# One-hot columns moved from GpSimd to VectorE and ScalarE, v tiles split one step earlier, rows fetched three slots ahead

## The chip, the cores and the metric

The kernel runs on one core of a Trainium2 chip. The metric is the device time of one execution in microseconds (us). The engines of the core run their own instruction queues in order and wait for each other through semaphores: TensorE (PE in the rows; PEld are its weight loads), VectorE (DVE), ScalarE (ACT), GpSimd (POOL), and SyncE (SP), which here only issues transfers. Sixteen DMA engines carry the transfers.

## What is computed

The reference is one layer of an encoder with 1024 tokens of width 1024: an attention group and an RWKV-7 group, their output projection, and a feed-forward part called PEER, which retrieves single-neuron experts by product keys. The change lies in PEER alone:

```python
# per token: 8 heads x 16 chosen experts = 128 indices ib and gates gb out of 128*128 experts
def block(args):                       # xc: 128 tokens, ic: their indices, gc: their gates
    xc, ic, gc = args
    u = jnp.take(expert_u, ic, axis=0)
    act = jax.nn.gelu(jnp.einsum('cd,ced->ce', xc, u), approximate=False)
    vv = jnp.take(expert_v, ic, axis=0)
    return jnp.einsum('ce,ced->cd', gc * act, vv)
```

## The kernel before

PEER is done in two ways side by side. For the first 3 blocks of 128 tokens (`NGB` = 3) the chosen rows of U and V are fetched from HBM by indirect DMA, one row for each token and slot: 384 slots, each one fetch `gu` and one fetch `gv` of 128 x 1024 fp32, issued by GpSimd (`fetch`, L1362). VectorE multiplies `gu` with the token's `ghr` and sums (L1390), and adds `gv` times the activation onto `gacc` (L1398), 16 slots later. For the other 5 blocks (640 tokens) all 16384 experts are computed densely, in 128 tiles of 128 experts: `act_half` makes the activations of a tile (48 matmuls, `pact`, L315 to L317), a gate zeroes those that were not chosen, and `v_steps` multiplies them with V. Each fp32 operand is split into a high part (ScalarE copy) and a low part (VectorE subtraction): `uTh`/`uTl`, `ah`/`al`, `vh`/`vl`, and each product is three matmuls.

**The gates stage** (`g_steps`) makes the gate tables. For each of 640 tokens, 128 slots on the partitions, `o2` is the one-hot of an expert's low 7 bits and `o1` the one-hot of its high 7 bits times its gate; the matmul `o1` by `o2` (L1733, `pgb`) is the token's 128 x 128 table of gates. One step `hot(t8)` makes the one-hots of 8 tokens, `mm(t8)` their 8 products; ScalarE evicts them into `st` (L1736), and SyncE stores `st` to `Gd` in HBM. There are 80 such steps, with two buffers (`NHOT` = 2) of `o1` and of `o2`. Before the change the 8 columns of `o1` are shared out by `MIX = "DDDDPPAA"`: four on VectorE and two on GpSimd (L1712, compare and multiply in one), two on ScalarE (L1718 and L1722, as relu(gate - gate * |x - index|)). `tT` holds the transposed indices and gates. Dense tiles (`A(e2, NEARLY)`) and 60 fetched slots (`NG3`) are laid between these steps.

**The last stage** goes over the 32 groups of 4 tiles. A group has 8 steps, one for each tile and half of the output (`one`): 15 matmuls `py` (L1827 to L1829) with `vh`, `vl`. After the last of 4 steps VectorE adds the 5 sums `py` onto `yac` (L1836), which frees their PSUM. In the same 8 steps the next group's activations are gated: `gate` multiplies `gl` by the table `gt_` on GpSimd (L1786), then come `ah` (ScalarE, L1787) and `al` (VectorE, L1788). Activations that were computed early come back from HBM (`gl<-actd`, L1776, SyncE), the others from `act_half`. `vr` tiles are loaded four steps ahead (`NVR` = 4 buffers), `vh` and `vl` have three buffers (`NV`). Fetches are tied behind GpSimd's latest gate or one-hot (`pace`).

The order of the instructions on each engine is not that of the code: a scheduler works it out before the run, from priorities in program order and estimated times, and from when buffers come free.

Of the kernel before, what the change touches and what calls it, by code (L numbers as in the profile page):

```python
# [8 lines left out]
F32 = mybir.dt.float32  # L9
# [4 lines left out]
AF = mybir.ActivationFunctionType  # L14
ALU = mybir.AluOpType
# [5 lines left out]
D = 1024  # L21
# [23 lines left out]
NPOP = 2  # L45
NHOT = 2
NXG = 3
LAG = 2
GD = 2
VAH = 0  # L50
NVR = 4
TRY = (1, 1)
WG = (1, 0, 0.99)
# [14 lines left out]
TC = 32  # L68
NSTB = 2
STQ = 0  # L70
MIX = "DDDDPPAA"
HD = 64


# [5 lines left out]
def body(tc, nc, I, out, dbg=None):  # L80
# [3 lines left out]
    with root:  # L84
# [76 lines left out]
        def acp(o_, i_):  # L161
            nc.scalar.activation(o_, i_, AF.Copy)  # L162
# [56 lines left out]
        for k in range(NK):  # L219
            for i in range(2):  # L220
                a = slot("adw")
# [10 lines left out]
        for tb in range(NB):  # L232
# [5 lines left out]
            if tb % 4 == 3:  # L238
                r_ = rstd[:, tb - 3:tb + 1]
# [1049 lines left out]
        for tb in range(NB):  # L1289
# [7 lines left out]
            if tb % 2:  # L1297
                r_ = ss2[:, tb - 1:tb + 1]
                nc.vector.tensor_scalar(r_, r_, 1.0 / D, 1e-6, op0=ALU.mult, op1=ALU.add)
                rsqrt(r_, r_, [128, 2], "r1")  # L1300
                for b in range(tb - 1, tb + 1):
                    h_ = tl[f"h{b}"]
                    for hf in range(2):
                        cs_ = slice(hf * 512, hf * 512 + 512)
                        nc.vector.scalar_tensor_tensor(h_[:, cs_], h2[b][:, cs_], ss2[:, b:b + 1], sc2[hf],
                                                       op0=ALU.mult, op1=ALU.mult)
# [113 lines left out]
        pace = [None]  # L1420
# [253 lines left out]
        with ES() as gs:  # L1674
# [7 lines left out]
            def g_steps(b):  # L1682
# [3 lines left out]
                def prep():  # L1686
                    ij = g1.tile([128, 2, 128], I32, name="ij", bufs=1)
                    nc.vector.tensor_scalar(ij[:, 0], eid[tb], 7, None, op0=ALU.logical_shift_right)
                    nc.vector.tensor_scalar(ij[:, 1], eid[tb], 127, None, op0=ALU.bitwise_and)
                    fj = g1.tile([128, 2, 128], F32, name="fj", bufs=1)  # L1690
                    nc.vector.tensor_copy(fj, ij)
                    pt = pg_.tile([128, 512], F32, name="ptg", tag="b")
                    nc.tensor.transpose(pt[:, 0:128], fj[:, 0], ident)
                    nc.tensor.transpose(pt[:, 128:256], fj[:, 1], ident)
                    nc.tensor.transpose(pt[:, 256:384], wgt[tb], ident)

                    s["t"] = tT = g1.tile([128, 5, 128], F32, name="tT")
                    acp(tT[:, 0:3].rearrange("p a b -> p (a b)"), pt[:, 0:384])
                    nc.scalar.activation(tT[:, 3], pt[:, 256:384], AF.Copy, scale=-1.0)
                    nc.scalar.activation(tT[:, 4], pt[:, 0:128], AF.Copy, scale=-1.0)  # L1700

                def hot(t8):
                    tT = s["t"]
                    t0 = t8 * 8
                    s[t8] = o1, o2 = [g1.tile([128, 8, 128], F32, name=n_, bufs=NHOT) for n_ in ("o1", "o2")]
                    nc.vector.tensor_tensor(o2, io128[:, None, :].to_broadcast([128, 8, 128]),
                                            tT[:, 1, t0:t0 + 8, None].to_broadcast([128, 8, 128]), ALU.is_equal)
                    for q in range(8):
                        t = t0 + q
                        if MIX[q] != "A":  # L1710
                            eng = nc.vector if MIX[q] == "D" else nc.gpsimd
                            r_ = eng.tensor_scalar(o1[:, q], io128, tT[:, 0, t:t + 1], tT[:, 2, t:t + 1],  # L1712
                                                   op0=ALU.is_equal, op1=ALU.mult)
                            if MIX[q] == "P":
                                pace[0] = r_
                        else:

                            nc.scalar.activation(o1[:, q], io128, AF.Abs, bias=tT[:, 4, t:t + 1])  # L1718
                    for q in range(8):
                        t = t0 + q  # L1720
                        if MIX[q] == "A":
                            nc.scalar.activation(o1[:, q], o1[:, q], AF.Relu, scale=tT[:, 3, t:t + 1],  # L1722
                                                 bias=tT[:, 2, t:t + 1])

                def mm(t8):
                    if t8 % (TC // 8) == 0:
# [189 lines left out]
```

## Time and profile before

| | |
|---|---|
| Median of 3 runs | 3918.12 us (3916.42 to 3923.77) |
| The profiled execution | 3917.25 us, span of its instructions 3915.5 us |
| Granted TensorE clock, mean | 0.925 |
| TensorE busy | 3337.0 us (85%) |
| VectorE busy | 3016.5 us (77%) |
| GpSimd busy | 1929.2 us (49%) |
| ScalarE busy | 1248.9 us (32%) |

Durations and waits come from the profiled execution. "Busy" is the time in which at least one instruction of the engine ran; matmuls are pipelined, so a busy TensorE is not one at its peak. A wait is put down to the instruction or the DMA that released it last.

### The profile page before, as it was taken

The numbers are of one execution on the slowest core, as the hardware profiler recorded it, in microseconds if no ns is written. First come the engines' busy times: TensorE is split into PE (matmuls) and PEld (weight loads), VectorE is DVE, ScalarE is ACT, GpSimd is POOL, SyncE is SP. The second block draws the span as 40 slices with busy tenths as digits, with TensorE's granted clock in tenths as the row PEclk, the third lists the DMA queues.
The fourth block names the chain that finished last, engine by engine and source line by source line (L and its number), as shares of the span: only waits on it lengthen the run. The fifth ranks groups of instructions, "written<-read, shape, count | busy, mean of one in ns | idle before, by whom it ended". The sixth has DMA issues, their size and how long they took to land. (4 is left out here: it accounts for less than half of the span.)

```text
span 3915.5 us, 59807 instructions
## 1 busy us (share of the span) xinstructions
PE 3337.0 (85%) x21937; PEld 2929.5 (75%) x21937; DVE 3016.5 (77%) x6210; ACT 1248.9 (32%) x2400; POOL 1929.2 (49%) x1506
## 2 busy tenths in 40 slices
PE   5968899899697978878778777898999889998898
PEld 4747877777586978878777776777777777777777
DVE  6785557667647899999988886777777877788776
ACT  3234344445213322222355552222222222222221
POOL 2132111221334365456799996555555655555541
PEclk9988999899798988998999898999999999999999
DMA  6443434443455366566688889777777877777774
GB/s 198 178 135 123 141 95 121 101 105 94 110 185 190 97 213 219 170 218 227 209 287 282 280 288 328 285 282 290 294 292 293 300 284 290 295 297 298 291 269 158
DMA packets 493454, 862.68 MB, mean 220 GB/s; under 512 B 149348, under 2 KB 290404, under 8 KB 489064
## 3 DMA queue, kind: packets, MB, share of 16 engines
q1 hardware_dynamic: 372840, 447.20, 35.3%
q0 software_dynamic: 113280, 411.63, 28.9%
q8 instruction: 173, 2.83, 0.3%
q10 hardware_dynamic: 7040, 0.03, 0.1%
q14 instruction: 121, 0.99, 0.1%
HBM read 741.91 MB, written 116.80 MB: 219 GB/s over the span
## 5 line engine op out<-in xcount | busy, mean ns | idle before, releaser
L317 PE MATMUL pact<-dTh,uTl 128*128 128x320 f32 x2048 | 650.3, 319 | 51.6 <-DVE uTl L1450 51.4
L315 PE MATMUL pact<-dTh,uTh 128*128 128x320 f32 x2048 | 652.6, 319 | 10.1 <-ACT gl L1461 6.1
L316 PE MATMUL pact<-dTl,uTh 128*128 128x320 f32 x2048 | 648.3, 317 | 0.0
L1390 DVE SCALAR_TENSOR_TENSOR gu<-gu,ghr 128x1024 f32<-128x1024 f32 x384 | 505.0, 1316 | 162.8 <-DMA gu<-in_peer_u_dram,ei 150.4
L1827 PE MATMUL py<-vh,ah 128*128 128x512 f32 x1280 | 523.7, 410 | 93.1 <-DVE yac L1836 64.3
L1398 DVE SCALAR_TENSOR_TENSOR gacc<-gv,gact,gacc 128x1024 f32<-128x1024 f32 x381 | 533.3, 1400 | 72.4 <-DMA gv<-in_peer_v_dram,ei 67.5
L1828 PE MATMUL py<-vl,ah 128*128 128x512 f32 x1280 | 527.6, 412 | 64.1 <-DVE vl L1807 63.5
L1362 POOL DMA_INDIRECT gu<-in_peer_u_dram,ei x384 | 504.0, 1313 | 123.6 <-issue 65.8
L1829 PE MATMUL py<-vh,al 128*128 128x512 f32 x1280 | 519.8, 406 | 3.7 <-DVE al L1788 3.7
L1362 POOL DMA_INDIRECT gv<-in_peer_v_dram,ei x384 | 457.4, 1191 | 131.4 <-issue 103.0
L317 PEld LDWEIGHTS pact<-dTh,uTl 128*128 128x128 f32 x2048 | 397.9, 195 | 58.3 <-DVE uTl L1450 58.2
L315 PEld LDWEIGHTS pact<-dTh,uTh 128*128 128x128 f32 x2048 | 398.9, 195 | 15.5 <-ACT gl L1461 8.0
L316 PEld LDWEIGHTS pact<-dTl,uTh 128*128 128x128 f32 x2048 | 398.6, 195 | 2.5
L1827 PEld LDWEIGHTS py<-vh,ah 128*128 128x128 f32 x1280 | 252.9, 198 | 154.9 <-issue 37.0
L1828 PEld LDWEIGHTS py<-vl,ah 128*128 128x128 f32 x1280 | 253.8, 198 | 140.0 <-DVE vl L1807 88.9
L1829 PEld LDWEIGHTS py<-vh,al 128*128 128x128 f32 x1280 | 253.5, 198 | 58.2 <-DVE al L1788 4.5
L1806 ACT ACTIVATE vh<-vr 128x512 fp32r<-128x512 f32 x256 | 156.0, 625 | 392.3 <-PE py L1829 361.9
L1733 PE MATMUL pgb<-o,o 128*128 128x128 f32 x1280 | 194.7, 300 | 80.7 <-POOL o L1712 76.8
L1712 POOL TENSOR_SCALAR o<-io,tT 128x128 f32<-128x128 f32 x160 | 244.5, 1533 | 11.7 <-ACT tT L162 9.3
L1733 PEld LDWEIGHTS pgb<-o,o 128*128 128x128 f32 x1280 | 174.3, 208 | 97.3 <-POOL o L1712 92.3
L1787 ACT ACTIVATE ah<-gl 128x640 fp32r<-128x640 f32 x128 | 91.2, 735 | 439.6 <-POOL gl L1786 302.9
L1788 DVE TENSOR_TENSOR al<-gl,ah 128x640 fp32r<-128x640 f32 x128 | 103.7, 830 | 130.3 <-ACT ah L1787 130.3
(1443 smaller groups left out, 7244.7 us busy)
## 6 DMA issues: line engine op xcount, KB each, us to landing
u<-in_peer_ut_dram SPq DMA_DIRECT2D x128, 512.0 KB
vr<-in_peer_v_dram SPq DMA_DIRECT2D x256, 256.0 KB
Gd<-st SPq DMA_DIRECT2D x160, 256.0 KB
actd<-gl SPq DMA_DIRECT2D x65, 320.0 KB
gl<-actd SPq DMA_DIRECT2D x65, 320.0 KB
awt<-in_ada_w_dram SPq DMA_DIRECT2D x32, 512.0 KB
wraw<-in_peer_w_query_dram SPq DMA_DIRECT2D x32, 512.0 KB
wraw<-in_w_in_dram SPq DMA_DIRECT2D x26, 512.0 KB
```

Of the source, the lines that this page charges most:

```text
L315: nc.tensor.matmul(ps, lh, rh, start=(i == 0), stop=False)
L316: nc.tensor.matmul(ps, lh, rl, start=False, stop=False)
L317: nc.tensor.matmul(ps, ll, rh, start=False, stop=(i == n - 1))
L1362: g_ = nc.gpsimd.indirect_dma_start(out=r_, out_offset=None, in_=src, in_offset=bass.IndirectOffsetOnAxis(ap=eid[tb][:, j:j + 1], axis=0))
L1390: nc.vector.scalar_tensor_tensor(u, u, 1.0, hr, op0=ALU.mult, op1=ALU.mult, accum_out=act[:, q:q + 1])
L1398: nc.vector.scalar_tensor_tensor(acc, v, pact[:, q:q + 1], acc, op0=ALU.mult, op1=ALU.add)
L1712: r_ = eng.tensor_scalar(o1[:, q], io128, tT[:, 0, t:t + 1], tT[:, 2, t:t + 1], op0=ALU.is_equal, op1=ALU.mult)
L1733: nc.tensor.matmul(pg[:, q * 128:(q + 1) * 128], o1[:, 4 * x_ + q], o2[:, 4 * x_ + q], start=True, stop=True)
L1806: nc.scalar.activation(vh, vts[i], AF.Copy)
L1827: nc.tensor.matmul(ys[hf][b], ah[:, ts], vh, start=(n == tiles[0]), stop=False)
L1828: nc.tensor.matmul(ys[hf][b], ah[:, ts], vl, start=False, stop=False)
L1829: nc.tensor.matmul(ys[hf][b], al[:, ts], vh, start=False, stop=(n == tiles[-1]))
```

## The change

Three things change. In the gates stage `MIX` goes: VectorE makes both one-hots of 8 tokens as whole comparisons, `o1` first, without the gates, and ScalarE then multiplies each of the 8 columns of `o1` by its gate (a copy with a pointer scale, in place). GpSimd makes no columns there, and so the fetches of that stage are no longer tied behind one. `tT` shrinks from five blocks to three. `VAH` = 1: in each step of the last stage the code splits the v tile of the next step. `LAG` = 3: the code fetches the rows of three slots ahead of the slot in work, with the buffers as they were (four of `gu` and of `gv`, three more in the gates stage).

```diff
--- before.py
+++ after.py
@@ -45,9 +45,9 @@
 NPOP = 2
 NHOT = 2
 NXG = 3
-LAG = 2
+LAG = 3
 GD = 2
-VAH = 0
+VAH = 1
 NVR = 4
 TRY = (1, 1)
 WG = (1, 0, 0.99)
@@ -68,7 +68,6 @@
 TC = 32
 NSTB = 2
 STQ = 0
-MIX = "DDDDPPAA"
 HD = 64
 
 
@@ -1694,33 +1693,19 @@
                     nc.tensor.transpose(pt[:, 128:256], fj[:, 1], ident)
                     nc.tensor.transpose(pt[:, 256:384], wgt[tb], ident)
 
-                    s["t"] = tT = g1.tile([128, 5, 128], F32, name="tT")
-                    acp(tT[:, 0:3].rearrange("p a b -> p (a b)"), pt[:, 0:384])
-                    nc.scalar.activation(tT[:, 3], pt[:, 256:384], AF.Copy, scale=-1.0)
-                    nc.scalar.activation(tT[:, 4], pt[:, 0:128], AF.Copy, scale=-1.0)
+                    s["t"] = tT = g1.tile([128, 3, 128], F32, name="tT")
+                    acp(tT.rearrange("p a b -> p (a b)"), pt[:, 0:384])
 
                 def hot(t8):
                     tT = s["t"]
                     t0 = t8 * 8
                     s[t8] = o1, o2 = [g1.tile([128, 8, 128], F32, name=n_, bufs=NHOT) for n_ in ("o1", "o2")]
-                    nc.vector.tensor_tensor(o2, io128[:, None, :].to_broadcast([128, 8, 128]),
-                                            tT[:, 1, t0:t0 + 8, None].to_broadcast([128, 8, 128]), ALU.is_equal)
+
+                    for i, o_ in enumerate((o1, o2)):
+                        nc.vector.tensor_tensor(o_, io128[:, None, :].to_broadcast([128, 8, 128]),
+                                                tT[:, i, t0:t0 + 8, None].to_broadcast([128, 8, 128]), ALU.is_equal)
                     for q in range(8):
-                        t = t0 + q
-                        if MIX[q] != "A":
-                            eng = nc.vector if MIX[q] == "D" else nc.gpsimd
-                            r_ = eng.tensor_scalar(o1[:, q], io128, tT[:, 0, t:t + 1], tT[:, 2, t:t + 1],
-                                                   op0=ALU.is_equal, op1=ALU.mult)
-                            if MIX[q] == "P":
-                                pace[0] = r_
-                        else:
-
-                            nc.scalar.activation(o1[:, q], io128, AF.Abs, bias=tT[:, 4, t:t + 1])
-                    for q in range(8):
-                        t = t0 + q
-                        if MIX[q] == "A":
-                            nc.scalar.activation(o1[:, q], o1[:, q], AF.Relu, scale=tT[:, 3, t:t + 1],
-                                                 bias=tT[:, 2, t:t + 1])
+                        nc.scalar.activation(o1[:, q], o1[:, q], AF.Copy, scale=tT[:, 2, t0 + q:t0 + q + 1])
 
                 def mm(t8):
                     if t8 % (TC // 8) == 0:
```

The scheduler's order shows what moves. **ScalarE in the gates stage**, in its second half; `o` are the one-hots, `st<-pgb` the evictions of the products, `gl<-pact` a dense activation. Before:

```order
L1736 ACTIVATE st<-pgb 128x128x4 x2
L1718 ACTIVATE o_21379<-io_11962,tT 128x128 x2
L1722 ACTIVATE o_21379<-o_21379,tT 128x128 x2
L1736 ACTIVATE st<-pgb 128x128x4 x2
L1718 ACTIVATE o_21412<-io_11962,tT 128x128 x2
L1722 ACTIVATE o_21412<-o_21412,tT 128x128 x2
L1736 ACTIVATE st<-pgb 128x128x4 x2
L1461 ACTIVATE gl<-pact 128x320
```
After the change:

```order
L1708 ACTIVATE o_21622<-o_21622,tT 128x128 x8
L1708 ACTIVATE o_21640<-o_21640,tT 128x128 x8
L1721 ACTIVATE st<-pgb 128x128x4 x4
L1460 ACTIVATE gl<-pact 128x320
L1708 ACTIVATE o_21700<-o_21700,tT 128x128 x8
L1708 ACTIVATE o_21726<-o_21726,tT 128x128 x8
L1721 ACTIVATE st<-pgb 128x128x4 x4
L1460 ACTIVATE gl<-pact 128x320
```
Four instructions on two columns become eight on eight columns, and two such groups stand behind each other more often, ahead of the evictions of both.

**VectorE in the last stage**, from the last `yac` of one half of a group to the row product behind the two `al` (buffer numbers tell a row: `gu_26924` is one fetch). Before:

```order
L1836 TENSOR_TENSOR yac4_22458<-yac4_22458,py_26675 128x512
L1807 TENSOR_TENSOR vl_26906<-vr_26746,vh_26905 128x512
L1390 SCALAR_TENSOR_TENSOR gu_26884,gact_26547<-gu_26884,ghr_22005 128x1024
L1398 SCALAR_TENSOR_TENSOR gacc_22926<-gv_26886,gact_25807,gacc_22926 128x1024
L1807 TENSOR_TENSOR vl_26941<-vr_26773,vh_26940 128x512
L1450 TENSOR_TENSOR uTl_27097<-u_26890,uTh_27096 128x1024
L1788 TENSOR_TENSOR al_26897<-gl_26805,ah_26896 128x640
L1788 TENSOR_TENSOR al_27000<-gl_26936,ah_26999 128x640
L1807 TENSOR_TENSOR vl_26970<-vr_26863,vh_26969 128x512
L1390 SCALAR_TENSOR_TENSOR gu_26924,gact_26547<-gu_26924,ghr_22005 128x1024
L1398 SCALAR_TENSOR_TENSOR gacc_22926<-gv_26926,gact_25807,gacc_22926 128x1024
```
After the change:

```order
L1821 TENSOR_TENSOR yac4_22372<-yac4_22372,py_26593 128x512
L1792 TENSOR_TENSOR vl_26784<-vr_26664,vh_26783 128x512
L1792 TENSOR_TENSOR vl_26824<-vr_26691,vh_26823 128x512
L1389 SCALAR_TENSOR_TENSOR gu_26802,gact_26465<-gu_26802,ghr_21927 128x1024
L1397 SCALAR_TENSOR_TENSOR gacc_22844<-gv_26804,gact_25725,gacc_22844 128x1024
L1449 TENSOR_TENSOR uTl_27015<-u_26808,uTh_27014 128x1024
L1773 TENSOR_TENSOR al_26815<-gl_26723,ah_26814 128x640
L1773 TENSOR_TENSOR al_26918<-gl_26854,ah_26917 128x640
L1792 TENSOR_TENSOR vl_26859<-vr_26781,vh_26858 128x512
L1389 SCALAR_TENSOR_TENSOR gu_26842,gact_26465<-gu_26842,ghr_21927 128x1024
L1397 SCALAR_TENSOR_TENSOR gacc_22844<-gv_26844,gact_25725,gacc_22844 128x1024
```
The second `vl` moves ahead of a pair of row products; what stands behind it is in the same order. The fetches of these rows on GpSimd, before:

```order
L1362 DMA gu_26884<-in_peer_u_dram,ei1_11947 128x1024
L1362 DMA gv_26886<-in_peer_v_dram,ei1_11947 128x1024
L1786 TENSOR_TENSOR gl_26936<-gl_26936,gt__26901 128x640
L1786 TENSOR_TENSOR gl_26805<-gl_26805,gt__26518 128x640
L1362 DMA gu_26924<-in_peer_u_dram,ei1_11947 128x1024
```
After the change:

```order
L1361 DMA gu_26802<-in_peer_u_dram,ei1_11947 128x1024
L1361 DMA gv_26804<-in_peer_v_dram,ei1_11947 128x1024
L1771 TENSOR_TENSOR gl_26854<-gl_26854,gt__26819 128x640
L1771 TENSOR_TENSOR gl_26723<-gl_26723,gt__26436 128x640
L1361 DMA gu_26842<-in_peer_u_dram,ei1_11947 128x1024
```
In both, the row that VectorE uses behind `al`, `al`, `vl` is the first one fetched behind the two gates `gl`.

**SyncE in the last stage**, the same group; `gl<-actd` loads an early activation. Before:

```order
L1439 DMA u_27094<-in_peer_ut_dram 128x1024
L1800 DMA vr_26863<-in_peer_v_dram 128x512
L1800 DMA vr_26903<-in_peer_v_dram 128x512
L1800 DMA vr_26938<-in_peer_v_dram 128x512
L1776 DMA gl_26936<-actd_11964 128x640
```
After the change:

```order
L1438 DMA u_27012<-in_peer_ut_dram 128x1024
L1785 DMA vr_26781<-in_peer_v_dram 128x512
L1785 DMA vr_26821<-in_peer_v_dram 128x512
L1785 DMA vr_26856<-in_peer_v_dram 128x512
L1785 DMA vr_26885<-in_peer_v_dram 128x512
L1761 DMA gl_26854<-actd_11964 128x640
```
One load of `vr` more stands ahead of the load of `gl`.

## Rows read from the trace of the kernel before

**Rows 1.** Windows of five stages, with the columns that their head names.

```profile
core 0: us, PE busy (x) PEld busy (x) DVE busy (x) ACT busy (x) POOL busy (x), PEclk, DMA share, GB/s
...
1381.00:1918.00 537.00, 441.15 (x2810) 432.45 (x2809) 529.36 (x1519) 131.87 (x225) 315.09 (x204) 0.92 0.64 213
1918.00:2349.00 431.00, 338.51 (x2226) 319.16 (x2226) 354.01 (x610) 239.17 (x557) 399.64 (x277) 0.91 0.86 276
2349.00:2370.00 21.00, 7.70 (x53) 7.44 (x51) 5.45 (x7) 2.51 (x4) 3.36 (x4) 0.78 1.02 337
2370.00:3916.00 1546.00, 1387.90 (x6792) 1190.03 (x6792) 1204.91 (x1556) 354.30 (x595) 845.16 (x639) 0.95 0.77 283
```

**Rows 2.** Groups by line, GpSimd, gates stage: busy us, mean ns | idle before.

```profile
L1712 POOL TENSOR_SCALAR o<-io,tT 128x128 f32<-128x128 f32 x160 | 244.5, 1533 | 11.7 <-ACT tT L162 9.3 <-issue 0.3
```

**Rows 3.** Waits in the gates stage: us in total, times, longest.

```profile
ACT st L1736 <- PE pgb L1733: 148.8, 115, 4.4
...
PE pgb L1733 <- POOL o L1712: 76.8, 68, 3.3
DVE o L1706 <- PE pgb L1733: 27.7, 22, 3.1
```

**Rows 4.** Waits in the last stage.

```profile
POOL gl L1786 <- DMA gl<-actd: 252.6, 22, 17.8
...
DVE gu L1390 <- DMA gu<-in_peer_u_dram,ei: 131.8, 42, 5.3
...
PE py L1827 <- DVE yac L1836: 64.3, 25, 5.1
PE py L1828 <- DVE vl L1807: 63.5, 48, 5.1
```

**Rows 5.** Timeline of GpSimd, one group of the last stage: start us, us.

```profile
2903.95 0.94 POOL L1362 DMA_INDIRECT gv<-in_peer_v_dram,ei  x1 [0.30 <-issue]
2921.37 1.56 POOL L1786 TENSOR_TENSOR gl<-gl,gt__26901 128x640 f32<-128x640 f32 x1 [16.48 <-DVE uTl L1450]
2922.89 1.56 POOL L1786 TENSOR_TENSOR gl<-gl,gt__26518 128x640 f32<-128x640 f32 x1
2924.60 0.97 POOL L1362 DMA_INDIRECT gu<-in_peer_u_dram,ei  x1 [0.15 <-issue]
```

**Rows 6.** Timeline of VectorE, the same group.

```profile
2915.88 0.67 DVE L1807 TENSOR_TENSOR vl<-vr,vh 128x512 fp32r<-128x512 f32 x1
...
2918.82 0.67 DVE L1807 TENSOR_TENSOR vl<-vr,vh 128x512 fp32r<-128x512 f32 x1
...
2925.25 1.56 DVE L1788 TENSOR_TENSOR al<-gl,ah 128x640 fp32r<-128x640 f32 x2 [4.63 <-ACT ah L1787]
2926.73 0.68 DVE L1807 TENSOR_TENSOR vl<-vr,vh 128x512 fp32r<-128x512 f32 x1
2932.36 1.22 DVE L1390 SCALAR_TENSOR_TENSOR gu<-gu,ghr 128x1024 f32<-128x1024 f32 x1 [4.94 <-DMA gu<-in_peer_u_dram,ei]
```

**Rows 7.** Groups by line, VectorE, gates stage.

```profile
L1712 DVE TENSOR_SCALAR o<-io,tT 128x128 f32<-128x128 f32 x320 | 100.2, 401 | 0.0
L1706 DVE TENSOR_TENSOR o<-io,tT 128x1024 f32<-128x1024 f32 x80 | 98.5, 1231 | 40.0 <-PE pgb L1733 27.7 <-issue 7.0 <-ACT tT L162 5.4
```

**Rows 8.** Groups by line, ScalarE, gates stage.

```profile
L1722 ACT ACTIVATE o<-o,tT 128x128 f32<-128x128 f32 x160 | 69.5, 483 | 0.0
L1718 ACT ACTIVATE o<-io,tT 128x128 f32<-128x128 f32 x160 | 54.8, 393 | 0.2
```

**Rows 9.** Timeline of ScalarE in the gates stage, two columns end to end.

```profile
2101.26 0.69 ACT L1718 ACTIVATE o<-io,tT 128x128 f32<-128x128 f32 x2
```

**Rows 10.** DMA of the gates stage.

```profile
DMA packets 103006, 118.75 MB, mean 276 GB/s; under 512 B 4946, under 2 KB 82770, under 8 KB 102972
```

**Rows 11.** Timeline of SyncE's queue, the group of rows 5 and 6.

```profile
2907.70 9.21 SPq L1800 DMA_DIRECT2D vr<-in_peer_v_dram  x3
2917.00 0.38 SPq L1776 DMA_DIRECT2D gl<-actd  x1
```

## The prediction

> **What bounds the kernel now.** I read the windows of the five stages first. The third, the gates stage (1918 to 2349 us), is the one whose code changes. Of its 431 us GpSimd is busy 399.64, or 93%, against 354.01 on VectorE, 338.51 on TensorE and 239.17 on ScalarE [rows 1]. GpSimd's one-hot columns alone are 244.5 us, 160 of them at 1533 ns [rows 2]; the rest is row fetches. The waits of the stage say the same: TensorE stood 76.8 us for a one-hot of GpSimd, ScalarE 148.8 us for TensorE, VectorE 27.7 us for TensorE [rows 3]. So here GpSimd sets the pace and the others wait behind it. The DMA engines come next: a share of 0.86 over these 431 us, 1.02 in the 21 us behind them, when the last stores drain [rows 1].
>
> The last stage (1546 us) is another case. TensorE is busy 1387.90 us of it and GpSimd only 845.16 [rows 1]. TensorE's waits there are 64.3 us for the sums `yac` and 63.5 us for `vl`, both VectorE's, and VectorE in its turn stood 131.8 us for fetched rows of U (42 times) while GpSimd's gates stood 252.6 us for loads of `gl` [rows 4]. One group of four tiles shows the loop. GpSimd's last fetch starts at 2903.95, then it waits 16.48 us at a gate, and the next row of U is asked for at 2924.60 [rows 5]. VectorE ran the two `al` of those gates at 2925.25 and one `vl` at 2926.73, then stood 4.94 us for that very row until 2932.36 [rows 6]. All that is queued behind it on VectorE, `yac` included, is late by as much, and TensorE waits for some of it.
>
> **The gates stage, cost by cost.** GpSimd loses all 160 columns: 399.64 - 244.5 = 155 us, no bound any more.
>
> VectorE gives up 320 single columns (100.2 us) and makes 80 whole comparisons more of the kind that it has (98.5 us for 80) [rows 7]. That is -1.7 us, so it stays at 352.
>
> ScalarE gives up 69.5 + 54.8 = 124.3 us [rows 8] and scales 640 columns of 128 in their place. The trace has no such copy of an SBUF column by a pointer scale. Nearest are `L1718`, one pointer operand, 393 ns, and `L1722`, two, 483 ns [rows 8]. Two of `L1718` end to end take 0.69 us [rows 9], so each after the first adds about 0.30. I take eight in a row as 0.393 + 7 x 0.297 = 2.47 us, 198 us for 80; the bounds are 640 x 0.297 = 190 and 640 x 0.483 = 309. ScalarE then has 239 - 124 + 198 = 313 us (305 to 424).
>
> TensorE's 338.51 us stay. The bytes stay too. DMA time is 0.86 x 431 = 371 us of all 16 engines.
>
> So with GpSimd out of the way the longest is DMA (371), then VectorE (352), TensorE (339), ScalarE (313), and the stretch must come out between 371 and 431. For how near one comes to a bound I have three rows: GpSimd 93% now, VectorE 529.36 of 537 us in the stage before, DMA 1.02 in the drain [rows 1]. I take 0.95 for DMA: 371 / 0.95 = 390 us, **-41 us** (0 to -74; the far end is VectorE as the bound at the 98.6% of the stage before, 352 / 0.986 = 357).
>
> What is queued behind the new work: ScalarE now stands between VectorE's `o1` and every product, and its order has one or two groups of eight copies and then the stores' evacuations, which wait for TensorE (front, first pair of order rows). One hot block takes one comparison (98.5 / 80 = 1.23 us), 2.47 us of copies and its eight products, and two blocks are in flight, over a period now of 431 / 80 = 5.4 us. That fits with room for a wait.
>
> The Trainium skill has a rule on the amount of DMA, in DMA: Bandwidth & Descriptors, Bandwidth: it puts the HBM limit of a core at about 358 GB/s. The stage moves 118.75 MB [rows 10]; by that figure the DMA floor would be an estimated 332 us, below VectorE's 352, and the sum would end at VectorE's bound, about 33 us lower than mine. No stretch in the rows here holds that rate (276 GB/s over the stage, 337 in the drain [rows 1]), so the busy share decides.
>
> **v tiles a step ahead.** The order puts the first two `vl` behind the sums `yac` next to each other (58 times, 12 before), so the second moves ahead of one pair of fetched-row products (front, second pair). In the group shown these two stood at 2915.88 and 2918.82 [rows 6]. But the next `vl` has the same work ahead of it as before, and so have the `yac`, and `vh` keeps its three buffers. A step of TensorE that waited for one of those waits as long: I put the gain at 0. Bounds: 63.5 us if all of TensorE's waits for `vl` went [rows 4], nothing if only the place of the wait moves.
>
> **Rows three slots ahead.** Fetches move one slot forward on GpSimd, but so do the products that use them on VectorE. In the order of before and of the change alike, the row used right behind `al`, `al`, `vl` is the one fetched first behind the two gates: 48 such places before, 48 after. That fetch still starts only when the gates have run, so the 4.94 us stay, at another slot's name. Gain 0; bounds: all of VectorE's 131.8 us for rows of U, of which TensorE could get back at most its 64.3 + 63.5 us [rows 4].
>
> **SyncE.** In 17 of 63 loads of `gl` the order has one more load of `vr` ahead (front, third pair). That load waits for a `vr` buffer, which the second `vl` of the pair frees. In the group shown the three `vr` loads held the queue 9.21 us and `gl` went out at 2917.00 [rows 11]. The second `vl` comes 0.6 us behind the first, a load takes about 0.33 more: 0.9 us later for the load, its gate, the fetch behind it and VectorE's product. 17 x 0.9 = 15 us if each were the last thing waited for; gates whose wait ended with that load are 22 [rows 4], about a third of the loads, so **+5 us** (0 to +15).
>
> **Sum.** 3917.25 (the profiled execution) - 41 + 5 = 3881; the median of the runs is 0.87 above the profiled one, so **3882 us**.
>
> **Rivals.**
> - *No gain, DMA is at its limit already.* The share is 0.86 of the stage, and packets may simply take longer when more engines are ready. Then the stretch stays near 425 us and the time near 3916. Against it: TensorE's wait for GpSimd is in the rows by name [rows 3], and the drain runs at 337 GB/s against 276 [rows 1].
> - *More gain.* DMA stretches as needed and VectorE sets the pace at 357 us: 3917 - 74 + 5 = 3849. The skill's bandwidth figure above speaks for this one. Or the shifted fetches do free VectorE's stalls, and TensorE gets back half of its 128 us of waits in the last stage: 3882 - 64 = 3818. Against the latter is the order: the stalled pair of fetch and use is the same.
> - *Slower: ScalarE in series.* ScalarE waits 148.8 us for TensorE now [rows 3]. If all of that stays beside 313 us of work, the stretch is 462 us, 31 more: 3917 + 31 + 5 + 1 = 3954. With the copies at 483 ns it is worse. It decides from waits above 431 - 313 = 118 us. Against it: 76.8 us of them are TensorE's own wait for GpSimd [rows 3], which goes; 72 are left, and 313 + 72 = 385 is below DMA's 390. A rule speaks for it: ScalarE: Activation LUTs, Rules for kernel authors, in the Trainium skill, would have a multiplication on VectorE, not on ScalarE. The trace shows its point: VectorE compared and scaled a column for 100.2 / 320 = 0.31 us in one instruction [rows 7], where it now takes 0.15 on VectorE and 0.31 on ScalarE.
>
> **How the numbers follow.** Forecast (3857 to 3908): 0.58. No gain (3908 to 3926): 0.16. More gain (below 3857): 0.13. Slower (above 3926): 0.13. What a measurement can tell from no change is about 0.2%, 7.8 us, so faster means below 3910: 0.58 + 0.13 + 0.03 of the no-gain case = 0.74; same 0.13; slower 0.13. The range holds the forecast, the VectorE-bound case and half of the no-gain one: 3838 to 3918.
>
> **What would show it.** Right: the stretch from the first comparison to the last product of the gates stage is 375 to 410 us; GpSimd is busy under 45% of it, the DMA share is over 0.92, the 640 copies come to about 200 us; in the last stage VectorE still has a 4 to 5 us wait for a row of U in nearly every group, and TensorE's waits for `yac` and `vl` stay within 20 us of 128. Wrong: a stage above 425 us with ScalarE busy or waiting throughout; a DMA share unchanged at 0.86 in a shorter stage (then DMA was not the bound); or a last stage that differs from 1546 us by more than 20.

## The result and the profile after

The changed kernel takes 3878.32 us (median of 4 runs, 3873.78 to 3885.51), the kernel before 3917.27 us beside it: a ratio of 0.9898, 95% interval 0.9880 to 0.9917. So it is 39 us faster, 4 us from the forecast. The profiled execution of after is the slowest of its four, 3885.51 us, and that of before took 3917.25; the 32 us between them are what the two traces can explain. The stages do not add up as the prediction had them.

First the windows of three stages, bounds set by the same events as in [rows 1]: first comparison of the gates stage, its last product, first `py`, end.

```profile
core 0: us, PE busy (x) PEld busy (x) DVE busy (x) ACT busy (x) POOL busy (x), PEclk, DMA share, GB/s
...
1916.00:2291.00 375.00, 312.15 (x2237) 302.32 (x2236) 340.96 (x368) 307.96 (x867) 194.81 (x113) 0.94 0.95 319
2291.00:2309.00 18.00, 7.54 (x51) 7.28 (x50) 9.77 (x13) 3.31 (x6) 2.71 (x3) 0.82 0.96 328
2309.00:3884.00 1575.00, 1391.50 (x6792) 1196.40 (x6791) 1199.30 (x1552) 353.31 (x594) 832.60 (x636) 0.95 0.75 278
```

Against [rows 1], the gates stage went from 431 to 375 us (-56), the drain from 21 to 18 (-3), and the last stage from 1546 to 1575 (+29); the start is 2 us earlier. That is -32. TensorE does the same in the last stage (1391.50 us busy, 1387.90 before), so 25 of the 29 us are idle time.

The groups of the gates stage: busy us and mean ns of one, then the idle time before them.

```profile
L1708 ACT ACTIVATE o<-o,tT 128x128 f32<-128x128 f32 x640 | 193.9, 392 | 18.8 <-DVE o L1705 18.7
L1705 DVE TENSOR_TENSOR o<-io,tT 128x1024 f32<-128x1024 f32 x160 | 186.9, 1217 | 28.7 <-ACT tT L161 17.0 <-PE pgb L1718 9.9 <-PE pact L314 1.9
...
L1361 POOL DMA_INDIRECT gv<-in_peer_v_dram,ei x56 | 101.7, 1816 | 39.8 <-DVE gacc L1397 24.0 <-DVE o L1705 9.4 <-issue 3.7
...
L1361 POOL DMA_INDIRECT gu<-in_peer_u_dram,ei x57 | 93.1, 1634 | 119.8 <-DVE gu L1389 113.3 <-DVE gacc L1397 4.3 <-issue 2.1
```

The waits of that stage (us in total, times, longest):

```profile
POOL gu L1361 <- DVE gu L1389: 113.3, 49, 10.9
...
PE pgb L1718 <- ACT o L1708: 24.7, 9, 10.6
ACT uTh L1448 <- DMA u<-in_peer_ut_dram: 24.1, 6, 10.4
...
DVE o L1705 <- ACT tT L161: 17.0, 5, 9.7
...
ACT st L1721 <- PE pgb L1718: 14.5, 30, 1.1
...
DVE o L1705 <- PE pgb L1718: 9.9, 3, 8.1
```

Its DMA traffic:

```profile
DMA packets 103193, 119.44 MB, mean 319 GB/s; under 512 B 4982, under 2 KB 82806, under 8 KB 103160
```

GpSimd now has time to wait, and the wait of ScalarE for TensorE is down from 148.8 us [rows 3] to 14.5. The bytes are those of [rows 10] to within 1%, moved at 319 GB/s where it was 276. GpSimd's long wait is for VectorE, which gives the buffers of the rows back.

The waits of the last stage, beside [rows 4]:

```profile
POOL gl L1771 <- DMA gl<-actd: 225.2, 18, 18.1
...
DVE gu L1389 <- DMA gu<-in_peer_u_dram,ei: 140.3, 45, 5.7
...
PE py L1813 <- DVE vl L1792: 71.9, 39, 5.2
PE py L1812 <- DVE yac L1821: 65.2, 25, 6.0
```

And VectorE in one group (start us, us), as in [rows 6]:

```profile
2869.59 1.56 DVE L1773 TENSOR_TENSOR al<-gl,ah 128x640 fp32r<-128x640 f32 x2 [3.75 <-ACT ah L1772]
2871.07 0.68 DVE L1792 TENSOR_TENSOR vl<-vr,vh 128x512 fp32r<-128x512 f32 x1
2876.37 1.23 DVE L1389 SCALAR_TENSOR_TENSOR gu<-gu,ghr 128x1024 f32<-128x1024 f32 x1 [4.62 <-DMA gu<-in_peer_u_dram,ei]
```

Two `al`, one `vl`, and then 4.62 us for a row of U: the same three instructions and the same stall, although the rows are fetched a slot earlier.

### The profile page after: what moved, and what is told of

Its sections match the earlier page's. It is cut to its first block, busy times and chain, and to the rows that moved or that the text cites. A ratio compares the mean times of both kernels' runs of the same rounds, so it can differ in the third digit from the quotient of the medians.

```text
span 3883.7 us, 59663 instructions
## 1 busy us (share of the span) xinstructions
PE 3309.9 (85%) x21937; PEld 2916.1 (75%) x21937; DVE 3001.6 (77%) x5970; ACT 1316.8 (34%) x2710; POOL 1723.4 (44%) x1346
## 5 line engine op out<-in xcount | busy, mean ns | idle before, releaser
L1361 POOL DMA_INDIRECT gu<-in_peer_u_dram,ei x384 | 516.6, 1345 | 283.6 <-DVE gu L1389 201.8
L1812 PE MATMUL py<-vh,ah 128*128 128x512 f32 x1280 | 527.7, 413 | 109.5 <-DVE yac L1821 65.2
L1389 DVE SCALAR_TENSOR_TENSOR gu<-gu,ghr 128x1024 f32<-128x1024 f32 x384 | 490.3, 1278 | 155.6 <-DMA gu<-in_peer_u_dram,ei 141.6
L1813 PE MATMUL py<-vl,ah 128*128 128x512 f32 x1280 | 528.9, 413 | 72.1 <-DVE vl L1792 71.9
L1361 POOL DMA_INDIRECT gv<-in_peer_v_dram,ei x384 | 486.9, 1268 | 148.9 <-issue 80.6
L1705 DVE TENSOR_TENSOR o<-io,tT 128x1024 f32<-128x1024 f32 x160 | 186.9, 1217 | 28.7 <-ACT tT L161 17.0
L1718 PE MATMUL pgb<-o,o 128*128 128x128 f32 x1280 | 174.5, 290 | 38.5 <-ACT o L1708 24.7
L1448 ACT ACTIVATE uTh<-u 128x1024 fp32r<-128x1024 f32 x128 | 135.1, 1056 | 205.4 <-PE pact L315 161.3
```

The lines of the kernel that those rows point to most:

```text
L1361: g_ = nc.gpsimd.indirect_dma_start(out=r_, out_offset=None, in_=src, in_offset=bass.IndirectOffsetOnAxis(ap=eid[tb][:, j:j + 1], axis=0))
L1389: nc.vector.scalar_tensor_tensor(u, u, 1.0, hr, op0=ALU.mult, op1=ALU.mult, accum_out=act[:, q:q + 1])
L1705: nc.vector.tensor_tensor(o_, io128[:, None, :].to_broadcast([128, 8, 128]), tT[:, i, t0:t0 + 8, None].to_broadcast([128, 8, 128]), ALU.is ...
L1718: nc.tensor.matmul(pg[:, q * 128:(q + 1) * 128], o1[:, 4 * x_ + q], o2[:, 4 * x_ + q], start=True, stop=True)
L1812: nc.tensor.matmul(ys[hf][b], ah[:, ts], vh, start=(n == tiles[0]), stop=False)
L1813: nc.tensor.matmul(ys[hf][b], ah[:, ts], vl, start=False, stop=False)
```

## The experiments

The kernel before took 3917 to 3921 us beside all of these, and ratios are to it. "Gates stage" is from the first comparison to the last product, "last stage" from the first `py` to the end, each in the profiled execution. For before they are 429.7 and 1545.1 us, for after 373.5 and 1575.0.

### One part at a time

The gates stage of the change alone:

```diff
-LAG = 3
+LAG = 2
 GD = 2
-VAH = 1
+VAH = 0
```

> Only the gates stage is changed; v tiles and fetch lag as before. In the changed kernel's profile the first product of the last stage starts 62 us earlier than before, but the last stage takes 30 us longer. Theory A (the two other edits cost the last stage 15 to 25 us through the queues of GpSimd and SyncE): this run is faster than the changed kernel by 15 to 25 us, about 3855 to 3863 us, with a last stage of 1546 to 1555 us. Rival B (the last stage is longer because of how the gates stage leaves it, or the two edits are worth nothing): 3874 to 3884 us, with a last stage of 1565 to 1577 us.

Measured: 3875.40 us (6 runs, 3859.72 to 3885.42), ratio 0.9884 (0.9859 to 0.9909). Gates stage 381.5 us, last stage 1549.0. The gates edit has the whole gain of the change. The time is the one that rival B named, the last stage the one that theory A named; what neither had is the stretch ahead of the gates stage, which begins at 1930.2 us here and at 1917.0 after the change.

The v tiles a step ahead, the third slot, and both, in the kernel before:

```diff
-VAH = 0
+VAH = 1
```

> Only the v tiles are split a step earlier. The prediction: no gain, up to 15 us lost by loads of gl that stand behind one more load of vr, 3917 to 3932 us. Theory A: 3922 to 3935. Rival B: 3915 to 3920. Rival C (the split really helps TensorE): 3870 to 3905.

```diff
-LAG = 2
+LAG = 3
```

> Only the fetches go three slots ahead. The prediction: 0, about 3917 us, with VectorE's wait for rows of U still at 125 to 145 us. Theory A (GpSimd then waits for buffers of rows and the gates behind it are late): 3925 to 3940. Rival C (fewer stalls): VectorE's wait under 90 us, 3880 to 3905.

```diff
-LAG = 2
+LAG = 3
 GD = 2
-VAH = 0
+VAH = 1
```

> Both edits of the last stage, the gates stage as before. Theory A: the sum of e2's and e3's losses, 3932 to 3942 us. Rival B: 3915 to 3922 us, and the 39 us of the changed kernel are the gates stage's alone.

| alone in the kernel before | us | ratio (95%) | gates stage | last stage |
|---|---|---|---|---|
| v tiles a step ahead | 3930.79 | 1.0032 (1.0019 to 1.0045) | 432.1 | 1559.5 |
| third slot | 3940.24 | 1.0057 (1.0037 to 1.0077) | 440.2 | 1562.5 |
| both | 3953.29 | 1.0082 (1.0063 to 1.0101) | 440.2 | 1572.0 |

Each of the two edits makes the kernel slower, by 14 and 17 us in the last stage, and the third slot by 10 more in the old gates stage, where GpSimd is the bound. In the new gates stage those 10 do not appear. Both together take 3953.29 us, above the 3932 to 3942 that theory A named; the loss of 34 us is that of the two apart (12 and 21). On top of the new gates stage the two edits together cost 3878.32 - 3875.40 = 3 us, less than the intervals of the two ratios can tell; in the profiled executions the last stage is 26 us longer (1549.0 to 1575.0) and the rest 22 us shorter, 13 of them ahead of the gates stage.

How far single stages can be trusted, the other traces tell. Four kernels here have both edits and no further one in the last stage: 1575.0, 1572.0, 1568.7 and 1562.8 us. The two with neither have 1545.1 and 1549.0. So the loss in the last stage is there each time, at 14 to 30 us. The gates stage of the change stands in six kernels, with 373.5 to 381.5 us.

The two edits are not apart in the scheduler's order. Counted in the traces, the first two `vl` behind the sums `yac` stand next to each other 12 times in the kernel before, 49 times with either edit alone and 58 times with both, and the loads of `gl` go out 17 places of `vr` later in all with either, 18 with both. So the third slot alone brings the shift in the order that was put down to the v tiles.

### What bounds the new gates stage

Without the scaling copies (the multiplication by the gates is left out):

```diff
-                    for q in range(8):
-                        nc.scalar.activation(o1[:, q], o1[:, q], AF.Copy, scale=tT[:, 2, t0 + q:t0 + q + 1])
```

> The changed kernel without the 640 scaling copies on ScalarE: the gates' multiplication is left out, everything else stays. It tells what bounds the new gates stage (373.5 us from its first comparison to its last product; DMA share 0.95, VectorE 341 us busy, ScalarE 308). If DMA bounds it, the stretch stays at 365 to 376 us and the DMA share at 0.95. If ScalarE or the chain VectorE, ScalarE, TensorE bounds it, the stretch falls to 345 to 360 us and the DMA share rises to 0.97 or more.

With one unused load more in each hot step:

```diff
+                    dm = g1.tile([128, 512], F32, name="dm", bufs=2)
+                    nc.sync.dma_start(dm, Ve[t8][:, 0:512])
```

> The changed kernel with one load of 256 KB more, unused, in each of the 80 hot steps of the gates stage: 21 MB beside the 119 that the stage moves. If DMA bounds the stage, its stretch grows in the same ratio, 373 x 140 / 119 = 439 us, so by 45 to 70 us. If large descriptors of SyncE's take less than their share of the time (21 MB at the 328 GB/s of the drain is 64 us, at twice that 32), the growth lies at 25 to 45. If DMA does not bound it, the growth is below 15 us and the DMA share rises above 1.0.

One execution of each (3869.79 and 3953.45 us). The gates stage without the copies, by its window:

```profile
1914.00:2287.00 373.00, 312.56 (x2250) 305.22 (x2249) 340.26 (x367) 131.82 (x227) 199.29 (x115) 0.93 0.96 320
```

and with the loads, by its window:

```profile
1913.00:2364.00 451.00, 322.42 (x2230) 312.83 (x2230) 340.40 (x366) 308.12 (x866) 190.20 (x113) 0.86 0.93 311
```

and by its DMA traffic:

```profile
DMA packets 114545, 140.10 MB, mean 311 GB/s; under 512 B 6247, under 2 KB 84071, under 8 KB 114511
```

176 us less work for ScalarE change the stage by 2 us, so ScalarE's work does not bound it. 20.7 MB more lengthen it by 76 us, above the 45 to 70 us that were expected if DMA bounds it, while VectorE's busy time stays at 340 us. In proportion to the bytes it would be 375 x 140.10 / 119.44 = 440 us; it is 451. But the loads bring more than bytes: they stand in SyncE's queue ahead of the kernel's own, and each waits for one of two buffers. SyncE's longest wait in this stage with the loads:

```profile
SPq L1703 <- DMA dm<-in_peer_v_dram: 123.2, 52, 8.6
```

and three of the other engines' waits:

```profile
ACT uTh L1448 <- DMA u<-in_peer_ut_dram: 76.9, 10, 16.3
...
DVE o L1707 <- PE pgb L1720: 66.1, 10, 16.5
...
DVE o L1707 <- ACT tT L161: 38.0, 4, 20.9
```

ScalarE waits 76.9 us for loads of `u`, not 24.1, and VectorE's two waits come to 104.1 us, not 26.9; the 77 us between are as long as the whole lengthening. Whether `u` is late because the DMA engines are full or because SyncE's queue is held up was not separated, so the test does not show that DMA bounds the changed kernel's stage.

The waits of the changed kernel speak for VectorE as much as for DMA. VectorE is busy 341 of 375 us, and its idle 34 us are the waits for ScalarE's `tT` (17.0), for TensorE (11.8) and for one load (5.3). It never waits for a fetched row there; GpSimd waits 113.3 us for VectorE instead. DMA shows by its share of 0.95 and by the 24.1 us that ScalarE waits for `u`. No run took work off VectorE, so which of the two is the nearer bound stays open.

The Trainium skill (DMA: Bandwidth & Descriptors, Bandwidth) puts a core's HBM limit at about 358 GB/s, half of what the two cores of a stack have. This stage holds 319 GB/s. The figure is no cap here: in the last version below, 100 us (2312.5 to 2412.5) run at 367 GB/s.

### Does the order hold the stall in place?

The prediction put the third slot at nothing because the order moves the use along with the fetch. That is tested by an order in which the use cannot move: the products of fetched rows are tied, on VectorE alone, behind the newest `vl`. Nothing is computed otherwise.

```diff
+        split_ = [None]
+        def behind(r_):
+            if split_[0] is not None:
+                tc.add_manual_dep(r_.ins, split_[0].ins.name,
+                                  mybir.DependencyInfo(mybir.DependencyClass.NoSync, mybir.DependencyReason.DATA),
+                                  reason="rows used behind the split of the step")
...
-                    nc.vector.scalar_tensor_tensor(u, u, 1.0, hr, op0=ALU.mult, op1=ALU.mult, accum_out=act[:, q:q + 1])
+                    behind(nc.vector.scalar_tensor_tensor(u, u, 1.0, hr, op0=ALU.mult, op1=ALU.mult, accum_out=act[:, q:q + 1]))
...
-                nc.vector.tensor_tensor(vl, vts[i], vh, ALU.subtract)
+                split_[0] = nc.vector.tensor_tensor(vl, vts[i], vh, ALU.subtract)
```

(`gacc` in the same way.) It ran in four forms. In the changed kernel:

> The changed kernel with one thing added: in the last stage VectorE's products of fetched rows (gu and gacc) are put behind the newest split vl of the step, in the order alone; nothing is computed otherwise. In the order the first fetch behind a gate was used right behind al and vl (0.7 us of VectorE's work later) in 46 places of the changed kernel; here it is in 0, and the use stands 10 us or more of work later. Theory A (the stall of VectorE for rows of U, 140 us in the changed kernel, is there because the order slides the use along with the fetch, so three slots ahead are worth as little as two): the stall falls below 70 us, TensorE's 137 us of waits for yac and vl fall by 20 to 60, the last stage comes from 1575 to 1515 to 1555 us, the time is 3820 to 3865 us. Theory B (the row buffers or the gates behind the rows set the pace): the stall moves to GpSimd (its waits for gu buffers, 43 us in the changed kernel, rise above 100), gates come later, the last stage stays within 10 us of 1575 and the time within 0.3% of 3878 us. Theory C (VectorE's products put back hold up yac and the gates al): the last stage is 10 to 40 us longer, 3890 to 3920 us.

there with `VAH = 0`:

> As the run before it in this call (products of fetched rows put behind the newest vl), but with the v tiles split where the kernel before has them (VAH 0). Here the first fetch behind a gate is used right behind al and vl in 5 places. Two readings of the 14 us that VAH alone cost in the last stage: if it is SyncE's, whose gl loads stand behind one more vr load with VAH 1, this kernel's last stage is 5 to 20 us shorter than that of the other one, and its TensorE waits for vl are no longer. If it is VectorE's second vl ahead of products, the order here gives that away anyway and the two kernels' last stages agree within 5 us.

there with `LAG = 2`:

> The changed kernel with the products of fetched rows behind the newest split vl, as in the run of 3687.86 us, but rows fetched two slots ahead again, not three. It tells what the third slot is worth once the order no longer slides the use along. In the order, two gates lie between fetch and use in 51 places here and in 103 with three slots; the first fetch behind a gate is used right behind al and vl in 2 places, against 0. Theory A (the distance from fetch to use is what counts): VectorE's wait for rows of U in the last stage, 8 us with three slots, is 20 to 70 us here, the last stage is 20 to 60 us longer than 1371.6, the time 3705 to 3750 us. Theory B (only the place of the products behind vl counts, the third slot is worth nothing): the last stage stays within 8 us of 1371.6 and the time within 0.3% of 3688.

and in the kernel before:

> The kernel before with one thing added: in the last stage the products of fetched rows are put behind the newest split vl. Old gates stage, v tiles split in their own step, rows two slots ahead. It tells whether the tie alone has the gain, without any part of the change. In its order the first fetch behind a gate is used right behind al and vl in 51 places, as many as before. If the distance from fetch to use counts, VectorE's wait for rows of U stays above 90 us, and the last stage is within 25 us of 1545: 3890 to 3925 us. If the tie alone does it, the last stage falls below 1450 us: under 3825 us.

| tied | us | ratio (95%) | last stage |
|---|---|---|---|
| before (old gates, `LAG` 2, `VAH` 0) | 3859.78 | 0.9844 (0.9831 to 0.9857) | 1479.1 |
| `LAG` 2, `VAH` 1 | 3741.45 | 0.9540 (0.9526 to 0.9554) | 1417.1 |
| `LAG` 3, `VAH` 0 | 3743.52 | 0.9554 (0.9531 to 0.9577) | 1425.6 |
| after (`LAG` 3, `VAH` 1) | 3687.86 | 0.9410 (0.9392 to 0.9428) | 1371.6 |

The window of the last stage of the changed kernel with the tie:

```profile
2317.00:3688.60 1371.60, 1327.92 (x6792) 1160.68 (x6792) 1215.09 (x1553) 353.80 (x594) 860.50 (x636) 0.99 0.85 319
```

its waits there:

```profile
POOL gl L1778 <- DMA gl<-actd: 116.1, 20, 9.0
...
POOL gu L1361 <- DVE gu L1389: 69.0, 53, 2.9
...
PE py L1820 <- DVE vl L1799: 17.4, 21, 3.3
...
DVE gu L1389 <- DMA gu<-in_peer_u_dram,ei: 8.2, 6, 2.6
```

and VectorE behind two gates of a group, with no stall in front of the product:

```profile
2854.28 1.56 DVE L1780 TENSOR_TENSOR al<-gl,ah 128x640 fp32r<-128x640 f32 x2 [3.75 <-ACT ah L1779]
2855.76 0.69 DVE L1799 TENSOR_TENSOR vl<-vr,vh 128x512 fp32r<-128x512 f32 x1
2856.37 1.22 DVE L1389 SCALAR_TENSOR_TENSOR gu<-gu,ghr 128x1024 f32<-128x1024 f32 x1
```

VectorE's wait for rows of U goes from 140.3 to 8.2 us, TensorE's wait for `vl` from 71.9 to 17.4, and its wait for `yac` from 65.2 to 0.9. Theory A had the direction and was far off in size: it allowed the last stage 1515 us at best. Of the 203 us, 140 are idle time of TensorE (1575.0 - 1391.5 = 183.5 before the tie, 43.7 with it); the other 64 are its busy time, for the same 6792 matmuls. Not all of the gain need be VectorE's: in the tied order the loads of `gl` also go out 28 places of `vr` earlier in all, 0.44 each, which by the slope found below would be some 10 us of the 203 (an estimate). The groups by line show it, for one of the three products; the changed kernel:

```profile
L1813 PE MATMUL py<-vl,ah 128*128 128x512 f32 x1280 | 528.9, 413 | 72.1 <-DVE vl L1792 71.9
```

and with the tie:

```profile
L1820 PE MATMUL py<-vl,ah 128*128 128x512 f32 x1280 | 505.7, 395 | 17.4 <-DVE vl L1799 17.4
```

One matmul takes 395 ns, not 413, and the granted clock of the stage is 0.99, not 0.95.

What the other three forms add: taking either edit out of the tied kernel costs some 55 us, although without the tie each cost time (3741.45 and 3743.52 with one of them, 3687.86 with both). What one is worth without the other was not run with the tie on the new gates stage. Both readings that were offered for the form with `VAH = 0` fell: its last stage is 54 us longer, not equal or shorter, and VectorE waits 63.5 us for rows of U there, not 8.2. By the code, with tiles split a step ahead the newest `vl` is that of the next step, so the tie pushes the products further back; the edit works through the tie there. For the third slot theory A held (3705 to 3750 us expected; VectorE's wait 62.3 us, 37 times). In the kernel before, the tie took 60 us off, between the two cases named: VectorE still waits 97.0 us for rows of U, yet TensorE's wait for `yac` is halved (33.0 us). So the distance is not all of it: the tie also puts `vl` and `yac` ahead of products that may stall. What each part is worth wasn't separated.

### SyncE's queue in front of `gl`

The one price that the prediction put on the v tiles was SyncE's: one more `vr` load ahead of some loads of `gl`. In the kernel with that edit alone, each `vr` load was put behind the newest `gl` load, in SyncE's order alone:

```diff
-                for i_ in range(i, i + NVR):
+                for i_ in range(i, i + NVR - 1):
                     v_load(i_)
...
-                nc.sync.dma_start(ats[n], actd[early.index(n)])
+                glq[0] = nc.sync.dma_start(ats[n], actd[early.index(n)])
...
+                    if g:
+                        v_load((g - 1) * 2 * GR + x_ * GR + y_ + NVR - 1)
...
+                    tc.add_manual_dep(r_.ins, glq[0].ins.name,
```

> The kernel with the v tiles split a step ahead as its only change (3930.79 us, 1.0032 of the kernel before), with SyncE's order turned: the vr load of the step stands behind the gl load, so that gl loads come 2.2 vr loads earlier than in the kernel before on average, not 0.27 later. VectorE's order is the same but for a few places. It tests the one price that was put on this edit, SyncE's queue. If the queue is what costs 14 us in the last stage, they come back: the last stage is at most 1550 us, the time at most 3920 us, and GpSimd's waits for gl loads fall below the 225 to 253 us of the kernels before and after. If the cost is VectorE's (the second vl ahead of products), the time stays at 3925 to 3940 us. If vr loads come too late instead, ScalarE's vh waits for vr and the time is above 3940; then this test says nothing.

Measured: 3880.63 us, ratio 0.9901 (0.9884 to 0.9918), against 1.0032 without the turn; last stage 1504.7 us, from 1559.5. SyncE's queue in one group (start us, us it holds the queue), first with the edit alone:

```profile
2913.47 9.81 SPq L1800 DMA_DIRECT2D vr<-in_peer_v_dram  x4
2923.33 0.42 SPq L1776 DMA_DIRECT2D gl<-actd  x1
```

then with the order turned:

```profile
2909.95 0.33 SPq L1778 DMA_DIRECT2D gl<-actd  x1
2910.32 10.08 SPq L1802 DMA_DIRECT2D vr<-in_peer_v_dram  x4
```

and the waits of its last stage:

```profile
ACT vh L1812 <- DMA vr<-in_peer_v_dram: 213.7, 53, 10.8
...
POOL gl L1788 <- DMA gl<-actd: 108.5, 14, 9.1
...
PE py L1834 <- DVE vl L1813: 99.0, 30, 5.0
```

The place in this queue is worth far more than the loss it was to explain: 55 us of last stage for gates whose loads go out 2.5 `vr` loads earlier (from 0.27 behind to 2.22 ahead), even though `vr` now comes late and TensorE waits 99.0 us for `vl`. That is some 22 us a load. By that slope 0.27 loads would be 6 of the 14 us that the edit costs; the rest has no cause shown.

The same turn by one load, in the tied kernel, is the best version found:

```diff
-                nc.sync.dma_start(ats[n], actd[early.index(n)])
+                glq[0] = nc.sync.dma_start(ats[n], actd[early.index(n)])
...
+                    tc.add_manual_dep(r_.ins, glq[0].ins.name,
```

> The version of 3687.86 us (the changed kernel, products of fetched rows behind the newest vl) with SyncE's order turned by one: each vr load stands behind the gl load of the step before, so that the loads of gl go out one vr load earlier on average. If SyncE's queue in front of gl still sets the gates there, GpSimd's 116 us of waits for gl loads fall below 80, the last stage falls from 1371.6 by 8 to 25 us and the time to 3663 to 3680 us. If the far use has made the gates uncritical (TensorE idles only 34 us in the last stage, 17 for vl, 10 for vh), the time stays at 3680 to 3696. If vr loads now come too late, ScalarE's vh waits for vr, TensorE waits more for vl and vh, and the time is above 3696.

Measured: 3653.70 us (5 runs, 3648.27 to 3660.71), ratio 0.9319 (0.9307 to 0.9332), 34 us below the tied kernel and below the range expected. The window of its last stage:

```profile
2320.00:3659.00 1339.00, 1313.98 (x6792) 1156.87 (x6792) 1262.97 (x1553) 359.09 (x595) 890.07 (x637) 0.99 0.87 327
```

and its waits:

```profile
ACT vh L1804 <- DMA vr<-in_peer_v_dram: 115.0, 25, 8.7
...
POOL gl L1780 <- DMA gl<-actd: 48.3, 14, 6.0
```

The gates wait 48.3 us for `gl`, not 116.1, and TensorE idles 25 of 1339 us, from 43.7 of 1371.6 (not 34, as the expectation had it). The 115.0 us that ScalarE waits for `vr` are covered.

## Why the prediction was right, and where it was not

**The gates stage: the first step right, the next bound not shown.** That GpSimd was the bound is shown: without its columns, and with the fetches no longer tied behind them, the stage is 48 us shorter with no other edit, and 48 to 56 in the six kernels that have it. The step behind it, "with GpSimd out of the way the longest is DMA", is not shown. The share came out at 0.95, the value chosen, but the stage's 375 us lie between the VectorE-bound case (357) and the DMA case (390), VectorE's waits name no row, and the added loads may have worked through SyncE's queue. The copies are 193.9 us (198 forecast), ScalarE 308 (313), VectorE 341 (352); TensorE's 338.51 us did not stay, they are 312.15, which bounds nothing. The term that was mis-sized is the one before the division: "DMA time is 0.86 x 431 = 371 us of all 16 engines", taken as fixed. It is 0.95 x 375 = 356 us for the same bytes; at the same share that is the difference between 390 and 375 us, and between -41 and -56. That the packets' time is no constant of the bytes shows in every trace: 369 to 372 us in the six with the old gates stage, 356 to 359 in the seven with the new one and no loads added, for 118 to 120 MB each. Why it is shorter stays open.

**The fetches on GpSimd.** "GpSimd is busy under 45%" was wrong: 194.81 of 375 us, 52%. The one-hots went, but the fetches left there take 1816 and 1634 ns, and with their waits GpSimd still is no bound.

**The last stage: the step that failed is "Gain 0" for two edits.** The third slot alone costs 17 us there, the v tiles 14, both 14 to 30. The prediction had the reason why they bring nothing, and it held: the stall behind `al`, `al`, `vl` is still there, 140.3 us (131.8 before), TensorE's waits for `vl` and `yac` come to 137 (within 20 of 128, as written), and when an order was made in which the use does not follow the fetch, 190 us more came off the median of the whole kernel. But "nothing" was taken from the waits that stay and not from what the shift itself delays. By the prediction's own line (within 20 us of 1546) the last stage of 1575 is outside. SyncE's +5 is the right size for its part, by the slope above, which is argued from one step of 2.5 loads and not measured at 0.27; the third slot alone brings as many places as the v tiles. The rest of the loss has no cause shown. For the third slot one more row differs: GpSimd waits 39.7 us for `gu` buffers with the slot alone, 24.5 in the kernel before. Whether that is the cause wasn't tried.

**The sum.** In the profiled execution 15 us too little gain in the gates stage and 24 too little loss in the last one set each other off, so that it lies 4 us from the forecast by luck, not by its terms. By the medians the terms look better, 44 us for the gates edit alone and 3 us back for the other two, but the stage windows do not bear that out: there the two other edits cost 26 us in the last stage, and the stretch ahead of the gates stage, which is no term of the sum, is 13 us shorter.

**The rivals.** No gain: out, the rate rose from 276 to 319 GB/s. VectorE as the bound at 357 us: the stage is 18 us above that, 15 below the DMA case; as a mechanism it is not out, since the stage is VectorE's 341 us of work and 34 us of waits. ScalarE in series: out, its waits for TensorE are 14.5 us, and the stage is no shorter without the copies, so the rule for a multiplication on VectorE (the Trainium skill, ScalarE: Activation LUTs, Rules for kernel authors) buys nothing in this place. Stalls freed by the shifted fetches (3818 us): out for the change as it stands; with the use tied it came, and was larger than its price.

## What to carry to other kernels

A prefetch is as deep as the order of the consumer leaves it: where a scheduler places both, look at the distance between fetch and use in its order, and tie the use if it slid along. A queue that issues loads in order is a resource like an engine; ask what stands in front of the load that the critical chain waits for. Where an edit costs time alone, try it again after the wait that hides it is gone: in the tied kernel taking either out costs some 55 us. A busy share near one does not name the bound by itself; look at which engine's waits name it.

## What the hardware showed unexpectedly

- The DMA engines' time for the same 119 MB was 371 us in a stage of 431 us that GpSimd bounded and 356 us in the one of 375 us.
- Issuing one fetch took GpSimd longer in the new gates stage: 1816 ns (`gv`) and 1634 ns (`gu`) on average at a DMA share of 0.95, against 1385 and 1269 ns at 0.86 in the kernel before. The share does not explain it alone: `gu` took 1439 ns in the stage ahead of the gates stage, at 0.64, and 1420 ns in the last stage of the best version, at 0.87. The cause is open. The gates stage of the kernel before has these two lines:

```profile
L1362 POOL DMA_INDIRECT gv<-in_peer_v_dram,ei x58 | 80.4, 1385 | 17.7 <-issue 14.9 <-DVE o L1712 1.2 <-DVE o L1706 0.9
L1362 POOL DMA_INDIRECT gu<-in_peer_u_dram,ei x59 | 74.8, 1269 | 10.0 <-issue 8.5 <-DVE o L1712 1.3 <-PE pgb L1733 0.2
```

- In the last stage the mean granted clock went from 0.95 to 0.99 with the tie (TensorE is granted 2.4 or 1.2 GHz; at 0.95 a tenth of the time is at the lower level, at 0.99 a fiftieth). TensorE's idle time had fallen from 183.5 to 43.7 us, and its busy time for the same matmuls fell by 64 us, some 56 of them by the ratio of the two clocks. The sum of the idle time does not settle the clock by itself: with SyncE's order turned and no tie TensorE idles 129 us and has 0.95, with the tie in the kernel before 117 us and 0.97.
